# A hybrid mLSTM and attention layer: other queues and another order for its first loads

## The chip, the cores and the metric

The kernel runs on one core of one Trainium2 chip. The metric is the device time of an execution in microseconds; three executions of the kernel before took 302.65, 302.69 and 302.83 us, median 302.69. The core has five engines with instruction streams of their own: TensorE (PE in the profile; its weight loads are shown apart as PEld), VectorE (DVE), ScalarE (ACT), GpSimd (POOL) and SyncE (SP). Transfers are issued by SP, by POOL or by ACT and carried out by 16 DMA engines.

## The reference

One layer of a decoder with 512 tokens and a model width of 1024, all in float32:

```
h    = RMSNorm(x) * norm_w
proj = h @ w_in                       # 1024 -> 4616 columns, ten parts
mlstm: causal conv + SiLU on q and k, chunked matrix memory with gates, per-head norm, SiLU gate z (4 heads x 128)
moba:  QK-norm, ALiBi, block-sparse causal attention, SiLU gate z (8 heads x 64)
out  = x + concat(mlstm, moba) @ w_out
```

What the change touches lies at the very start: the first columns of `proj`, for which `x` (transposed) and the first weights have to be in on-chip memory.

## The kernel before

**Products in three parts.** Every float32 matrix is split into a high part (cast to the fp32r type, `whi` or `xh`) and the rest (`wlo` or `xl`). A product is three products on PE: high with high, `wlo` with `xh`, `whi` with `xl`. For the first weights, ACT makes `xh` as a copy scaled by `norm_w` (a column of the tile `sm`), DVE makes `xl` from the same raw tile, the same column and `xh`, and DVE makes both `whi` and `wlo` (later weights get `whi` from ACT). This is `split_x` and `g_split` with the loop over `kk` in lines 675 to 684; `kk = 0` is done in two halves, k = 0 and k = 1.

**The first stage.** The chunk called z (520 columns) is computed for all 512 tokens. Its order (line 1138) runs over k, 128 rows of the contraction each; for each k over the three part products; for each of these over four token tiles, two products each, one of 264 columns and one of 256. So a group is eight products on PE, and three groups make a k: (`whi`, `xh`), (`wlo`, `xh`), (`whi`, `xl`). Behind this stage follow the q and k projections by a scheme with seven block products instead of eight (m1 to m7), then the other projections mixed with the mLSTM and the attention work, then the output projection.

**The first loads.** `xraw` holds the transposed x in four tiles of two halves; `load_x(kk, u)` (line 642) loads half u of tile kk, 256 KB, and `load_w` (line 502) loads one piece of weights, with `between` as two halves of 260 KB with something else issued between them. All go through SP. The raw x tiles lie in `tq` and `tk`, which are used for something else later. `smalls` (31 KB: `norm_w`, convolution weights, gate biases and the like) goes into the tile `sm`.

**Warm-up and constants.** Ahead of all that, DVE clears a small matrix `zero` and a column `warm`, ACT runs one SiLU on `warm` (which brings a table load), and PE multiplies `zero` with itself ten times (lines 448 to 452). POOL scales one column of `sm` (line 594), then makes the identity `ident`, distances and other constants; DVE makes `sel`, four selection matrices of 36 x 128, from `ident` (lines 625 to 628).

**What sets the order.** Instructions given before `nc.on = True` (line 647) are issued in the order of the code, each on its engine. After that line the class `Schedule` collects every instruction with its engine, an estimated cost (`cost`, line 220) and its predecessors (by overlapping regions), and `issue` (line 348) places them by list scheduling: `place` gives each engine, when it is free, the most urgent instruction that is ready; urgencies come from a pass backwards through the graph; of the program order and twelve such rounds the order with the smallest planned span is taken. In this reckoning a transfer is an issue on SP (100 ns in `cost`), then a task on one resource `dma` at 1480 ns per 512 KB with a reserve factor of 1.5, then 3500 ns of latency; DVE and ACT costs have a factor of 1.06, a result passes to another engine in 400 ns, and on the same engine in 110 ns. What was issued before `nc.on` is not part of the graph and counts as there from the start.

Of the kernel before, what the change touches and what calls it, by code (L numbers as in the profile page):

```python
# [12 lines left out]
F32R = mybir.dt.float32r  # L13
AF = mybir.ActivationFunctionType
ALU = mybir.AluOpType
AX = mybir.AxisListType

P = 128
D = 1024
S = 512  # L20
NT = S // P
KT = D // P
MLH = 4
# [4 lines left out]
C_NW, C_CW, C_CB, C_MN, C_QW, C_KW, C_GB = 0, 8, 40, 48, 52, 53, 54  # L28
# [103 lines left out]
class Stage:  # L132
# [6 lines left out]
    def add(self, eng, cost, fn, after=(), at=0.0, lat=220.0, then=0.0):  # L139

        t = {"eng": eng, "cost": cost, "fn": fn, "after": [a for a in after if a], "at": at, "lat": lat,
             "then": then, "n": len(self.tasks)}
        self.tasks.append(t)
        return t
# [45 lines left out]
class Schedule:  # L190
# [29 lines left out]
    def cost(self, eng, name, out, ins, args, kw):  # L220
        n = 1
        for d in (args[1] if name == "tensor_reduce" else out).shape[1:]:
            n *= d
        if name.startswith("dma"):
            return 1000.0 if eng == "gpsimd" else 100.0
        if eng == "tensor":
            if name == "transpose":
                return 109.0
            n = 1
            for d in kw["rhs"].shape[1:]:  # L230
                n *= d
            if kw["rhs"].dtype == F32R:

                return (max(0.452 * n, 60.0) + 2.0) * (0.5 if kw["rhs"].shape[0] == 64 else 1.0)
            return max(n, 64) * 4 * (0.43 if out.shape[0] == P else 0.21)
        if eng == "scalar":
            c = 180.0 + 0.85 * n
            if name == "activation":
                c += 95.0 * sum(isinstance(kw.get(k), bass.AP) for k in ("scale", "bias"))
            return c + (190.0 if "accum_out" in kw else 0.0)  # L240
        if eng == "gpsimd":
            return 330.0 + 190.0 * n if kw.get("op") == ALU.pow else 500.0 + 1.05 * n
        if name == "tensor_tensor_scan":
            return 1210.0
        if name == "tensor_copy" and not any(r[0].startswith("bank") for r in ins):
            return 160.0 + 0.52 * n
        c = 155.0 + 1.04 * n
        if name == "scalar_tensor_tensor" and len(ins) > 2:
            c += 100.0
        return c + (83.0 if "accum_out" in kw else 0.0)  # L250
# [137 lines left out]
def hybrid_layer(ctx: ExitStack, tc: tile.TileContext, xT, x, w_in, w_out, smalls, out):  # L388
    nc = Schedule(tc.nc)
# [10 lines left out]
    def sb(name, shape, dtype=F32):  # L400
        return const.tile(shape, dtype, name=name)
# [35 lines left out]
        return tinies[:, ntiny[0] - n:ntiny[0]]  # L437

    sm = sb("sm", [P, NSMALL])
    nc.sync.dma_start(sm, smalls)  # L440


    rstdb = sb("rstdb", [P, S])
# [1 line left out]
    zero = rstdb[:, 0:256].bitcast(mybir.dt.bfloat16)  # L445
    warm = sb("warm", [P, 1])
    nc.vector.memset(warm, 0.0)
    nc.scalar.activation(warm, warm, AF.Silu)
    wb = banks.get()
    for _ in range(10):  # L450
        nc.tensor.matmul(wb, lhsT=zero[:, 0:P], rhs=zero, start=True, stop=True)
    banks.put(0.0, wb)

# [2 lines left out]
    for name, cols in _chunks():  # L456
        n = len(cols)
# [31 lines left out]
    def raw_room():  # L489
        turn["raw"] += 1  # L490
        return rawroom[(turn["raw"] - 1) % 3]
# [4 lines left out]
    def in_src(name, kk, n=512):  # L496
        return bass.AP(tensor=w_in.tensor, offset=w_in.offset + offs_w[name, kk], ap=[[2 * n, P], [1, 2 * n]])

    def pair(t, n):
        return t[:, :2 * n].rearrange("p (k n) -> p k n", k=2)  # L500

    def load_w(dst=None, between=None):
        if not lseq or (dst is None and nout[0] >= 3):
            return
        i = lseq.pop(0)
        name, kk, n = pieces[i][:3]
        if dst is None:
            nout[0] += 1
            dst = raw_room()
        src = in_src(name, kk, n)  # L510
        if between:
            nc.sync.dma_start(dst[:, :n], src[:, :n])
            between()
            nc.sync.dma_start(dst[:, n:2 * n], src[:, n:])
        else:
            nc.sync.dma_start(dst[:, :2 * n], src)
        raws[i] = (dst, pair(dst, n))
# [73 lines left out]
        plan.until(lambda: (name, kk) in W)  # L591
        return W[name, kk]

    nc.gpsimd.tensor_scalar(sm[64:128, C_QW:C_QW + 1], sm[64:128, C_QW:C_QW + 1], 2.0, 0.0, op0=ALU.mult, op1=ALU.add)


    ident = sb("ident", [P, P])
    make_identity(tc.nc, ident)
# [9 lines left out]


    sz = sb("sz", [P, NT, 512])  # L610
    tq = sb("tq", [P, NT, 512])
    tk = sb("tk", [P, NT, 512])
    vbuf = sb("vbuf", [P, NT * MLH * 129])
    tv = vbuf[:, :NT * 512].rearrange("p (t n) -> p t n", t=NT)
    mv = vbuf.rearrange("p (t h e) -> p t h e", t=NT, h=MLH)
# [6 lines left out]
    emcol = sb("emcol", [P, NT, 4])  # L622
    mrow2 = sb("mrow2", [36, S], F32R)
    nc.gpsimd.memset(mrow2.bitcast(F32), 0.0)
    sel = sb("sel", [36, MLH, P], F32R)
    for h in range(MLH):
        nc.vector.tensor_tensor(sel[:, h], ident[0:36, h:h + 1].to_broadcast([36, P]),
                                ident[0:36, 32 + h:33 + h].to_broadcast([36, P]), op=ALU.add)
    xpt = sb("xp", [P, 2, S + 4])
    nc.gpsimd.memset(xpt[:, :, 0:3], 0.0)  # L630
    xps = Bufs(plan, [xpt[:, i] for i in range(2)])
# [2 lines left out]
        return cv[c // 2][:, c % 2] if c < 4 else tq[:, c - 4]  # L634


    flat = lambda ap: ap.rearrange("p a n -> p (a n)")
    xraw = [flat(tq)[:, 0:1024], flat(tq)[:, 1024:2048], flat(tk)[:, 0:1024], flat(tk)[:, 1024:2048]]
    xtok = [vbuf[:, 1024 * (t % 2):1024 * (t % 2) + 1024] for t in range(NT)]
    zb = [b5.get() for _ in range(4)]  # L640

    def load_x(kk, u):
        nc.sync.dma_start(xraw[kk][:, u * 512:(u + 1) * 512],
                          bass.AP(tensor=xT.tensor, offset=xT.offset + kk * P * 1024 + u * 512,
                                  ap=[[1024, P], [1, 512]]))

    nc.on = True
    load_x(0, 0)
    load_w(zb[0], lambda: load_x(0, 1))
    for kk in range(1, 4):  # L650
        load_w(zb[kk])
        for u in range(2):
# [22 lines left out]
    for kk in range(4):  # L675
# [6 lines left out]
        for _ in split:  # L682
            pass
        nsplit[0] += 1
    xtmp = [t[:, 0:1024] for t in zb]
    plan.now = act.clock = dve.clock = 5500.0


# [429 lines left out]
    def pe_task(cost, fn, after=()):  # L1118
        nonlocal pe_last
        pe_last = st.add("PE", cost, fn, [pe_last, *after], lat=0.0)  # L1120
        return pe_last
# [100 lines left out]
    for m in PAIR:  # L1222
        for j in range(8):
            a, k = (j // 4, j % 4) if m in ("m6", "m7", "m4") else (j % 2, j // 2)
# [181 lines left out]
    for r in range(2):  # L1406
        for c in range(2):
            t = b5.get()
# [81 lines left out]
    for n, name in enumerate(NAMES):  # L1490
        if name not in SUMS:
            continue
        tag, other, op = SUMS[name]
# [136 lines left out]
```

## Time and profile before

| | us |
|---|---|
| profiled execution, whole | 302.68 |
| its span, first to last instruction | 301.0 |
| median of three runs | 302.69 |
| PE busy | 296.0 (98% of the span) |
| DVE busy | 214.9 (71%) |
| ACT busy | 169.6 (56%) |
| POOL busy | 67.1 (22%) |
| share of PE in the chain that ended last | 97% |

How to read it: busy time counts the execution of instructions, not waits and not the issue of transfers. The span begins with the first recorded instruction, so 1.68 us of the execution lie outside it. Matmuls are pipelined and their ends are modelled, so the start of a matmul or of a weight load is a safer number than its end. The chain is followed back from the last instruction to whatever released each step.

### The profile page before, as it was taken

The page shows a single profiled execution, that of the slowest core. Times are in us where ns is not written, and L with a number is a line of the kernel's source. Part 1 is how long each engine was busy: PE and PEld are TensorE (multiplying, and loading weights), DVE is VectorE, ACT ScalarE, POOL GpSimd, SP SyncE. Part 2 cuts the span into 40 slices and gives each one's busy share as a digit, 9 for nine tenths or more (in the row PEclk, how much of TensorE's full clock was granted, in tenths as well). Part 3 has the DMA queues.
Part 4 walks back from the last instruction along what each step waited for, and adds up shares of the span by engine and source line. Part 5 has one row for each costly group of instructions (what it writes and reads, how often), then busy time and mean ns, then how long its engine had stood idle before and what let it go on. Part 6 is the DMA issues. An engine that isn't in the chain of part 4 may idle for free.

```text
span 301.0 us, 4348 instructions
## 1 busy us (share of the span) xinstructions
PE 296.0 (98%) x1566; PEld 234.9 (78%) x1566; DVE 214.9 (71%) x457; ACT 169.6 (56%) x309; POOL 67.1 (22%) x90
## 2 busy tenths in 40 slices
PE   8999999999999999999999999999999999999995
PEld 3999888888887667767776668888889988888884
DVE  4886996789697675986686784372046767899992
ACT  3685749875537854364554599377032525779500
POOL 4000202149900344002561031000101037121200
PEclk9999999999999999999999999999999999999998
DMA  7994785643134200240001601465518399964434
GB/s 203 396 415 186 191 237 148 121 138 114 58 111 140 71 2 0 70 142 1 1 3 70 209 2 70 70 207 154 131 42 212 102 286 255 247 112 74 71 127 153
DMA packets 13381, 40.19 MB, mean 134 GB/s; under 512 B 1584, under 2 KB 1840, under 8 KB 13360
## 3 DMA queue, kind: packets, MB, share of 16 engines
q1 hardware_dynamic: 10640, 32.05, 30.6%
q0 software_dynamic: 2720, 7.87, 15.3%
q8 instruction: 12, 0.20, 0.3%
q14 instruction: 9, 0.07, 0.1%
HBM read 37.81 MB, written 2.10 MB: 133 GB/s over the span
## 4 chain that ended last, share of the span: by engine, by line
PE 97%; DMA 1%; DVE 0%; SPq 0%; issue 0%
PE bank L258 97%; DMA b<-in_w_in_dram 1%; DVE whi L258 0%; DVE b L258 0%; SPq L258 0%; SPq L381 0%
## 5 line engine op out<-in xcount | busy, mean ns | idle before, releaser
L258 PE MATMUL bank<-wlo,xh 128*128 128x512 f32 (+2 forms) x220 | 71.3, 358 | 0.0
L258 PE MATMUL bank<-whi,xl 128*128 128x512 f32 (+2 forms) x220 | 71.1, 359 | 0.0
L258 PE MATMUL bank<-whi,xh 128*128 128x512 f32 (+2 forms) x220 | 70.9, 362 | 0.1
L258 DVE TENSOR_TENSOR wlo<-raw,whi 128x1024 fp32r<-128x1024 f32 x35 | 42.5, 1218 | 22.3 <-ACT whi L258 22.2
L258 PEld LDWEIGHTS bank<-whi,xh 128*128 128x128 f32 x220 | 38.1, 188 | 8.1 <-ACT xh L258 1.0
L258 PEld LDWEIGHTS bank<-wlo,xh 128*128 128x128 f32 x220 | 38.3, 188 | 6.6 <-issue 0.2
L258 PEld LDWEIGHTS bank<-whi,xl 128*128 128x128 f32 x220 | 38.3, 188 | 6.4
L258 ACT CAST whi<-raw 128x1024 fp32r<-128x1024 f32 x35 | 36.5, 1049 | 11.6 <-PE bank L258 11.5
L258 PE MATMUL bank<-xh,whi 128*128 128x512 f32 x96 | 40.8, 425 | 0.0
L258 PE MATMUL bank<-xl,whi 128*128 128x512 f32 x96 | 39.4, 410 | 0.0
L258 PE MATMUL bank<-xh,wlo 128*128 128x512 f32 x96 | 38.7, 403 | 0.0
L258 PE MATMUL bank<-whi,br 128*128 128x512 f32 x112 | 35.9, 397 | 0.0
L258 POOL TENSOR_SCALAR b<-b,tinies 128x128 f32<-128x128 f32 (+3 forms) x32 | 20.0, 632 | 35.1 <-DVE tinies L258 32.5
L258 PEld LDWEIGHTS bank<-whi,br 128*128 128x128 f32 x112 | 21.0, 188 | 5.0
L258 ACT ACTIVATE b<-b,tinies 128x128 f32<-128x128 f32 (+3 forms) x32 | 17.8, 556 | 11.3 <-DVE tinies L258 11.0
L258 DVE CUSTOM_DVE_ANT_0 b<-bank,b 128x128 f32<-128x128 f32 (+3 forms) x32 | 14.8, 483 | 10.7 <-PE bank L258 10.7
L258 PEld LDWEIGHTS bank<-xh,whi 128*128 128x128 f32 x96 | 18.1, 188 | 5.5 <-issue 1.4
L258 PE MATMUL bank<-wlo,br 128*128 128x512 f32 x56 | 22.2, 400 | 0.0
L258 PEld LDWEIGHTS bank<-xh,wlo 128*128 128x128 f32 x96 | 18.1, 188 | 3.8 <-issue 0.2
L258 PEld LDWEIGHTS bank<-xl,whi 128*128 128x128 f32 x96 | 18.1, 189 | 3.6 <-issue 0.7
L258 POOL TENSOR_TENSOR tinies<-tinies,mhalf 128x8 f32<-128x8 f32 (+1 forms) x12 | 18.9, 1589 | 6.3 <-DVE tinies L258 6.2
L258 PE MATMUL bank<-ident,b 128*128 128x128 f32 (+1 forms) x104 | 19.0, 267 | 0.0
(170 smaller groups left out, 457.2 us busy)
## 6 DMA issues: line engine op xcount, KB each, us to landing
raw<-in_w_in_dram SPq DMA_DIRECT2D x28, 512.0 KB, 3.4
raw<-in_w_out_dram SPq DMA_DIRECT2D x5, 512.0 KB, 4.4
vbuf<-in_x_dram SPq DMA_DIRECT2D x4, 512.0 KB, 7.8
out_dram<-b SPq DMA_DIRECT2D x7, 256.0 KB, 2.1
b<-in_w_in_dram SPq DMA_DIRECT2D x3, 520.0 KB, 7.1
raw<-in_w_out_dram POOLq DMA_DIRECT2D x3, 512.0 KB, 6.3
b<-in_x_dram POOLq DMA_DIRECT2D x6, 256.0 KB, 4.4
tq<-in_xT_dram SPq DMA_DIRECT2D x4, 256.0 KB, 4.9
```

Source lines behind the costliest of these rows:

```text
L258: call = lambda: fn(*args, **kw)
```

## The change

Five edits, all in the first loads. The first x tile half is issued from ScalarE before the SiLU, ahead of the planner's part. On SP the first half of the first weights comes first in the code, then `smalls`, the second x half and the second half of the weights; all other loads follow as before. The POOL instruction on `sm` and the building of `sel` move behind `nc.on = True`, so that the planner places them. Eight warm-up products are issued instead of ten. And the planner's cost of issuing a DMA on an engine other than GpSimd is 450 ns instead of 100, for the whole kernel. `tq`, `tk`, `flat` and `xp` are only declared at another place, and an unused name goes.

```diff
-            return 1000.0 if eng == "gpsimd" else 100.0
+            return 1000.0 if eng == "gpsimd" else 450.0
...
     sm = sb("sm", [P, NSMALL])
-    nc.sync.dma_start(sm, smalls)
...
     nc.vector.memset(warm, 0.0)
+    tq, tk = sb("tq", [P, NT, 512]), sb("tk", [P, NT, 512])
+    flat = lambda ap: ap.rearrange("p a n -> p (a n)")
+    nc.scalar.dma_start(flat(tq)[:, 0:512], bass.AP(tensor=xT.tensor, offset=xT.offset, ap=[[1024, P], [1, 512]]))
     nc.scalar.activation(warm, warm, AF.Silu)
     wb = banks.get()
-    for _ in range(10):
+    for _ in range(8):
         nc.tensor.matmul(wb, lhsT=zero[:, 0:P], rhs=zero, start=True, stop=True)
...
-    nc.gpsimd.tensor_scalar(sm[64:128, C_QW:C_QW + 1], sm[64:128, C_QW:C_QW + 1], 2.0, 0.0, op0=ALU.mult, op1=ALU.add)
-
     ident = sb("ident", [P, P])
...
+    nc.on = True
+    load_w(zb[0], lambda: (nc.sync.dma_start(sm, smalls), load_x(0, 1)))
     sel = sb("sel", [36, MLH, P], F32R)
     for h in range(MLH):
         nc.vector.tensor_tensor(sel[:, h], ident[0:36, h:h + 1].to_broadcast([36, P]),
                                 ident[0:36, 32 + h:33 + h].to_broadcast([36, P]), op=ALU.add)
...
-    nc.on = True
-    load_x(0, 0)
-    load_w(zb[0], lambda: load_x(0, 1))
     for kk in range(1, 4):
         load_w(zb[kk])
         for u in range(2):
...
+    nc.gpsimd.tensor_scalar(sm[64:128, C_QW:C_QW + 1], sm[64:128, C_QW:C_QW + 1], 2.0, 0.0, op0=ALU.mult, op1=ALU.add)
     plan.now = act.clock = dve.clock = 5500.0
```

## Rows read from the trace of the kernel before

**Rows 1.** Chain that ended last, in order of time: start us, us, what

```profile
1.70 3.43 DMA b<-in_w_in_dram
...
5.16 0.54 DVE whi L258
...
5.83 291.52 PE bank L258 x1556
```

**Rows 2.** Waits of PE's weight loads, whole span: us in total, times, longest us

```profile
PEld bank L258 <- issue: 12.0, 42, 0.8
PEld bank L258 <- DVE tinies L258: 1.8, 5, 0.4
...
PEld bank L258 <- ACT b L258: 1.4, 4, 0.4
```

**Rows 3.** SP from 0 to 18 us: start, us, instruction, count, idle before and releaser

```profile
0.79 0.39 SPq L381 DMA_DIRECT2D sm<-in_smalls_dram  x1
1.24 0.42 SPq L258 DMA_DIRECT2D tq<-in_xT_dram  x1
1.70 0.42 SPq L258 DMA_DIRECT2D b<-in_w_in_dram  x1
```

**Rows 4.** ACT from 0 to 18 us

```profile
0.79 1.28 ACT L381 ACT_TABLE_LOAD   x1 [0.79 <-PEq L1618]
...
4.55 0.72 ACT L258 ACTIVATE xh<-tq,sm 128x512 fp32r<-128x512 f32 x1 [2.27 <-DMA tq<-in_xT_dram]
5.84 0.72 ACT L258 ACTIVATE xh<-tq,sm 128x512 fp32r<-128x512 f32 x1 [0.57 <-DMA tq<-in_xT_dram]
9.69 1.43 ACT L258 ACTIVATE xh<-tq,sm 128x512 fp32r<-128x512 f32 x2 [3.12 <-DMA tq<-in_xT_dram]
```

**Rows 5.** DVE from 0 to 18 us

```profile
3.52 0.89 DVE L381 TENSOR_TENSOR sel<-ident 36x128 fp32r<-36x128 f32 x4 [2.33 <-POOL ident masks.py:199]
5.16 0.53 DVE L258 CAST whi<-b 128x520 fp32r<-128x520 f32 x1 [0.74 <-DMA b<-in_w_in_dram]
5.61 0.73 DVE L258 SCALAR_TENSOR_TENSOR xl<-tq,sm,xh 128x512 fp32r<-128x512 f32 x1
6.26 0.69 DVE L258 TENSOR_TENSOR wlo<-b,whi 128x520 fp32r<-128x520 f32 x1
...
9.05 0.70 DVE L258 CAST whi<-b 128x1040 fp32r<-128x1040 f32 x1 [0.48 <-DMA b<-in_w_in_dram]
```

**Rows 6.** PE from 0 to 18 us: products, merged by group

```profile
1.24 4.45 PE L381 MATMUL bank<-rstdb 128*128 128x512 bf16 x10 [1.24 <-DVE warm L381]
5.83 1.24 PE L258 MATMUL bank<-whi,xh 128*128 128x264 f32 x8
7.01 1.22 PE L258 MATMUL bank<-wlo,xh 128*128 128x264 f32 x8
8.07 1.12 PE L258 MATMUL bank<-whi,xl 128*128 128x264 f32 x8
...
11.91 1.12 PE L258 MATMUL bank<-whi,xh 128*128 128x264 f32 x8
```

**Rows 7.** DMA issues by line: count, size of one, median us from issue to landing

```profile
sm<-in_smalls_dram SPq DMA_DIRECT2D x1, 31.0 KB, 1.8
```

**Rows 8.** PE's weight loads from 0 to 18 us, the third and the tenth

```profile
1.65 0.15 PEld L381 LDWEIGHTS <-rstdb 128*128 128x128 bf16 x1 [0.28 <-issue]
...
4.63 0.15 PEld L381 LDWEIGHTS <-rstdb 128*128 128x128 bf16 x1 [0.28 <-issue]
```

**Rows 9.** Windows: us, busy (count) of PE, PEld, DVE, ACT, POOL, PEclk, DMA share, GB/s

```profile
0.00:5.83 5.83, 4.45 (x10) 1.37 (x11) 1.84 (x8) 2.21 (x3) 3.04 (x14) 1.00 0.61 179
...
20.00:25.00 5.00, 5.00 (x43) 5.00 (x43) 2.76 (x7) 1.47 (x3) 0.00 (x0) 1.00 1.03 418
```

**Rows 10.** POOL from 0 to 18 us

```profile
2.68 0.18 POOL L381 TENSOR_SCALAR sm<-sm 64x1 f32<-64x1 f32 x1 [2.18 <-DMA sm<-in_smalls_dram]
```

**Rows 11.** The tile sel: its readers, ns min/median/max, first to last start us

```profile
L258 PEld LDWEIGHTS bank<-mrow,sel x4: 182/183/186, 170.7 to 172.7; 36*128 36x128 f32 x4
```

More of the change, by code (lines that the diff above doesn't have):

```diff
@@ L610, in hybrid_layer @@
     sz = sb("sz", [P, NT, 512])
-    tq = sb("tq", [P, NT, 512])
-    tk = sb("tk", [P, NT, 512])
     vbuf = sb("vbuf", [P, NT * MLH * 129])
@@ L624, in hybrid_layer @@
     nc.gpsimd.memset(mrow2.bitcast(F32), 0.0)
[L625 to L628, printed above, removed]
     xpt = sb("xp", [P, 2, S + 4])
@@ L634, in cvt @@
         return cv[c // 2][:, c % 2] if c < 4 else tq[:, c - 4]
-    flat = lambda ap: ap.rearrange("p a n -> p (a n)")
     xraw = [flat(tq)[:, 0:1024], flat(tq)[:, 1024:2048], flat(tk)[:, 0:1024], flat(tk)[:, 1024:2048]]
@@ L647, in hybrid_layer @@
     nc.on = True
-    load_x(0, 0)
-    load_w(zb[0], lambda: load_x(0, 1))
+    load_w(zb[0], lambda: (nc.sync.dma_start(sm, smalls), load_x(0, 1)))
+    sel = sb("sel", [36, MLH, P], F32R)
+    for h in range(MLH):
+        nc.vector.tensor_tensor(sel[:, h], ident[0:36, h:h + 1].to_broadcast([36, P]),
+                                ident[0:36, 32 + h:33 + h].to_broadcast([36, P]), op=ALU.add)
     for kk in range(1, 4):
@@ L684, in hybrid_layer @@
         nsplit[0] += 1
-    xtmp = [t[:, 0:1024] for t in zb]
+    nc.gpsimd.tensor_scalar(sm[64:128, C_QW:C_QW + 1], sm[64:128, C_QW:C_QW + 1], 2.0, 0.0, op0=ALU.mult, op1=ALU.add)
     plan.now = act.clock = dve.clock = 5500.0
```

## The prediction

> **What bounds the kernel now.** I read the chain of waits in order of time first. One unbroken PE piece runs from 5.83 us for 291.52 us of the 301.0, and what stands ahead of it is a DMA issue, 3.43 us of a transfer and one DVE cast [rows 1]. Then I looked for waits inside the piece: the table of what PE's weight loads waited for has no transfer in it, only small items, 3.2 us in 9 pieces for DVE and ACT results beside 12.0 us for which no engine is named [rows 2]. So PE's stream of products is a block of fixed length behind a start-up, and any change to the start-up is worth what it moves the block.
>
> Next I read the start-up engine by engine. SP issues one DMA every 0.46 us: `sm` at 0.79, the first x tile at 1.24, the first half of the first weights at 1.70, and the second x tile in the slot after [rows 3]. The x tile has landed when ACT begins its cast `xh`, at 4.55, the second when the next begins, at 5.84 [rows 4]. The weights land at 5.13 (1.70 + 3.43), DVE casts `whi` from 5.16 to 5.69 [rows 1, 5], and the first product stands at 5.83, 0.14 us later [rows 6]. `xh` was done at 5.27, so the weights decided. The first group of eight products (`whi`, `xh`) is followed at 7.01 by the second (`wlo`, `xh`), and the groups then settle at one every 0.96 us (four of them from 8.07 to 11.91, [rows 6]). The second group came later than 5.83 + 0.96 = 6.79, because DVE finished `wlo` at 6.95: it had put `xl` (5.61 to 6.34) ahead of it [rows 5]. The real anchor of the block is thus 7.01.
>
> **The change part by part.** The time of the profiled execution is 302.68 us, 1.68 more than its span, and the median of the runs is 302.69, so I sum against 302.68.
>
> *Weights first on SP.* Issue goes from 1.70 to 0.79, 0.91 us earlier. If the transfer takes its 3.43 us again, it lands at 4.22. But x tile and weights now start at the same moment, and before they needed 3.89 us together (1.24 to 5.13): at worst 0.79 + 3.89 = 4.68. Both ends come from [rows 1, 3]; I take the middle, 4.45.
>
> *The x tile from ScalarE's queue.* ACT's first instruction, a table load, starts at 0.79 [rows 4]; the DMA issue goes ahead of it and costs ACT some 0.42 us (SP's row for one DMA, [rows 3]). The table load then ends near 2.5 instead of 2.07, a small activation behind it; ACT idles until 4.55 today, so that is hidden, and would cost only if the data came before that. The tile lands between 4.10 (0.45 earlier) and 4.68.
>
> *`sm` behind the weights.* This is the edit with a price. `xh` and `xl` are scaled by columns of `sm`, which today lies ready at 2.59 (0.79 + 1.8, [rows 7]), and which is now issued at about 1.25, behind 260 KB of weights. Alone it would be there at 3.05; treated like the second x tile, which landed 0.71 after the weights ahead of it (5.84 less 5.13), at 5.16. By size (31 of 256 KB of that 0.71, hence 0.09) I take 4.45 + 0.09 = 4.54, nearest to that row scaled. The Trainium skill's page "DMA: Bandwidth & Descriptors", section "Queues, rings and completion order", says that each DMA engine works off one queue's descriptors in ring order and alternates between the queues that have work. No row here shows two hardware queues at once; by it `sm` waits for all the weights ahead of it while the x tile shares with them, which would put all three at about 4.68 to 4.77 and the gain 0.2 us below mine.
>
> *First product.* ACT casts `xh` from 4.54 to 5.26 (0.72, [rows 4]); `whi` is ready at 4.48 + 0.53 = 5.01, so ACT, not DVE, is late now. With the same 0.14 us to PE: 5.40, or 0.43 earlier.
>
> *The second group.* The planner that orders the instructions puts `xl` ahead of `wlo` today because in its own reckoning the x tile is there 1.1 us before the weights and `wlo` must wait 110 ns behind `whi`, while `xl` is ready. With the x tile out of the plan and `sm` behind the weights it reckons `whi` done at 5.53, `wlo` ready at 5.64, `xl` at 6.36, so `wlo` goes first. Then `wlo` is done at 5.01 + 0.69 = 5.70, before it is wanted at 5.40 + 0.96 = 6.36. The gain there is 7.01 - 6.36 = 0.65. Should `xl` stay first: 5.26 + 0.73 + 0.69 = 6.68, plus the 0.06 to PE, 6.74: 0.27.
>
> *Eight warm-up products.* Ten run from 1.24 to 5.69 [rows 6], 0.426 apart (seven steps of their weight loads from 1.65 to 4.63, [rows 8]); eight end 0.85 earlier, at 4.84. With ten, PE could not have begun at 5.40, so this edit makes the gain possible. What it risks is the clock. The granted clock reads 1.00 in the start-up too [rows 9], but 512 columns in 0.426 us are 1.2 GHz, and products of 264 columns in 0.12 us (0.96 for eight) are 2.4 GHz. The tenth warm-up product still started at the slow level (near 5.07) and the real ones at 5.83 were fast: the rise lay between. Where it lies late in that stretch, my first products run slow until then: at most 0.43 us at half speed, 0.2; I charge 0.05.
>
> *`sel` later, and the POOL scaling of `sm`.* Four DVE instructions (0.89 us) at 3.52 wait for `ident`, which POOL makes only after waiting until 2.68 for `sm` [rows 5, 10]. Without that wait `ident` is there some 1.9 us earlier and `sel` ends well before 4.4. Its first reader is at 170.7 [rows 11]. Cost nothing; if it landed behind `whi` it would cost 0.89 of DVE in the only stretch where DVE is close. The moved POOL instruction takes 0.18 us [rows 10], and POOL then has nothing in the window from 20 to 25 us [rows 9], so it hides.
>
> *What is late next.* Every later load keeps its place in SP's order and is issued one slot (0.46) earlier. The seventh group (k = 2) starts at 11.91 and had `whi` at 9.75, both kept waiting by transfers, `xh` at 10.41 [rows 4 to 6]: 1.5 us of slack, more than any gain here, and its transfers move too. The stream keeps the DMA engines full to 25 us [rows 9], so it shifts as a whole.
>
> *The planner's 450 instead of 100 ns per SP DMA* can reorder instructions in the whole kernel. Its bounds are the waits of PE that exist, 3.2 us in 9 pieces of up to 0.4 [rows 2]: one more or one less, +-0.4.
>
> Sum: -0.65 + 0.05 = -0.60, so 302.68 - 0.60 = 302.08. Bounds from the parts: weights and `sm` at 4.22 and 4.31 give 5.17, 6.13 and a gain of 0.88; `sm` at 5.16 gives 6.02, 6.98 and a gain of 0.03, below nothing with the clock's 0.2.
>
> **The rivals.**
> 1. *The clock rises late.* The warm-up stops at 4.84, before the rise of today (after 5.07), and PE then idles until 5.40, where the gap was 0.14. If the chip wants its activity anew, the products run at 1.2 GHz from 5.40 for as long as the rise took from 1.24, 3.83 to 4.59 us. A group takes 8 x 264/1.2 = 1.76 instead of 0.96, so 46% of that is lost: 1.75 to 2.1. Time: 302.08 + 1.75 to 2.1, about 304.0, slower. It decides from where the rise needs the last two products. For it: ten products were still slow. Against: PE is busy from 1.24 to 4.84 and again from 5.40. The Trainium skill's page "TensorE: Matmul & The Clock Gate", section "What's actually happening", states that "the default state is throttled, and activity releases the throttle"; the trace agrees (slow at 1.24, fast at 5.83), and whether eight products are activity enough no row here shows.
> 2. *`sm` takes the place of the wait removed*, or `xl` stays ahead of `wlo`: gain 0 to 0.3, 302.4 to 302.7. For it: `sm` is 31 KB over 128 partitions, so many small packets, and no row shows such a tile behind a full queue. Against: it is an eighth of an x tile.
> 3. *The change doesn't do what it says*: ACT's table load (1.28) stays ahead of its DMA. Issue at 2.1, tile at 5.4, `xh` at 6.1, second group at 7.2: +0.2, 302.9. Against: the load belongs to the activation behind it.
> 4. *Another order later in the kernel* gives or takes a wait or two: 301.6 or 302.8.
>
> **How the numbers follow.** Forecast 0.60, with its own range 301.7 to 302.5; rival 1 0.18; rival 2 0.13; rival 3 0.03; rival 4 0.06. About 0.2% (0.6 us, so 302.09 and 303.29) is what a measurement of this kernel can tell from no change, and the forecast sits at that edge: a little over half of it counts as faster (0.35), since its bounds leave about as much on either side; rival 4's better half and the luckier part of rival 2's uncertain price make it 0.40. Slower is rival 1 and a little of 4: 0.20. Same takes 0.40. The range reaches from 301.6 to 303.9, into rival 1, leaving out its dearer part.
>
> **What would show it.** Right: an ACT DMA at 0.79 and SP's weights at 0.79; `xh` beginning near 4.5 and just behind the landing of `sm`; `wlo` ahead of `xl` on DVE; first product near 5.4, second group near 6.36, groups 0.96 apart at once; and the PE block as long as before (291.5). Wrong: products of 264 columns 0.22 apart behind 5.4 (rival 1); `xh` at 5 or later with ACT waiting for `sm` (rival 2); the ACT DMA behind 2 us (rival 3); a PE block of another length (rival 4).

## The result, and the profile after

The changed kernel takes 305.15 us (median of eight executions), the kernel before 302.74 beside it: ratio 1.006, interval 1.0031 to 1.0089. It is slower, where 302.08 was forecast. The eight executions fall into two groups with nothing between them: three at 303.12 to 303.21 and five at 305.13 to 305.49. The profiled execution took 305.49, 2.81 more than that of before, with a span of 303.8.

The start of the new order came as planned. SP and ACT from 0 to 9 us (start, us, instruction, idle before and releaser), to be held against [rows 3, 4]:

```profile
0.79 0.39 SPq L258 DMA_DIRECT2D b<-in_w_in_dram  x1
1.23 0.42 SPq L258 DMA_DIRECT2D sm<-in_smalls_dram  x1
```

```profile
0.79 0.41 ACTq L381 DMA_DIRECT2D tq<-in_xT_dram  x1
1.22 1.28 ACT L381 ACT_TABLE_LOAD   x1 [1.22 <-PEq L1614]
...
4.70 1.50 ACT L258 ACTIVATE xh<-tq,sm 128x512 fp32r<-128x512 f32 x2 [1.98 <-DMA sm<-in_smalls_dram]
```

The x tile's DMA stands ahead of the table load, `xh` now waits for `sm`, and on DVE `wlo` stands ahead of `xl`, against [rows 5]:

```profile
4.23 0.43 DVE L258 CAST whi<-b 128x520 fp32r<-128x520 f32 x1 [1.95 <-DMA b<-in_w_in_dram]
4.70 0.73 DVE L258 TENSOR_TENSOR wlo<-b,whi 128x520 fp32r<-128x520 f32 x1
5.45 0.75 DVE L258 SCALAR_TENSOR_TENSOR xl<-tq,sm,xh 128x512 fp32r<-128x512 f32 x1
```

The products are another matter. PE from 0 to 18 us, merged by group, against [rows 6]:

```profile
1.24 3.60 PE L381 MATMUL bank<-rstdb 128*128 128x512 bf16 x8 [1.24 <-DVE warm L381]
5.47 2.10 PE L258 MATMUL bank<-whi,xh 128*128 128x264 f32 x8 [0.63 <-DVE wlo L258]
7.37 1.94 PE L258 MATMUL bank<-wlo,xh 128*128 128x264 f32 x8
9.10 1.80 PE L258 MATMUL bank<-whi,xl 128*128 128x264 f32 x8
10.74 1.14 PE L258 MATMUL bank<-whi,xh 128*128 128x264 f32 x8
...
16.51 1.11 PE L258 MATMUL bank<-whi,xh 128*128 128x264 f32 x8
```

The first product is at 5.47, 0.36 earlier than before (its releaser is given as `wlo`, done at 5.43; what it needs is `xh`, done at 5.42). But the first three groups start 1.90, 1.73 and 1.64 us apart and only the later ones 0.96. The window table, its columns as in [rows 9], has for the slow stretch:

```profile
5.47:10.70 5.23, 5.23 (x24) 5.23 (x25) 5.01 (x8) 2.39 (x4) 0.01 (x1) 1.00 1.00 367
```

24 products in 5.23 us are 0.218 each; 264 or 256 columns in 0.218 us are 1.2 GHz. The column of the granted clock (the last but two) reads 1.00 all the same. It did so in the slow start-up of before, too [rows 9]; the level there has to be read from the pace of the products. The tenth group starts at 16.51, and at 14.79 in the trace of before: 1.72 us later.

The rest is lost far from the edit. The chain that ended last, which before held one unbroken PE piece [rows 1]:

```profile
0.79 3.42 DMA b<-in_w_in_dram
...
5.47 261.84 PE bank L258 x1409
...
267.81 0.90 issue
268.71 1.05 ACT whi L258
...
271.57 1.08 DVE wlo L258
...
275.74 2.29 DVE wlo L258 x2
...
278.07 22.09 PE bank L258 x106
```

PE's block ends at 300.16 instead of 297.35, so 2.81 later in all: 1.72 by the tenth group and 1.09 behind it, of which 0.90 is one wait of PE for `wlo`:

```profile
278.07 0.51 PE L258 MATMUL bank<-wlo,xh 128*128 128x512 f32 x1 [0.90 <-DVE wlo L258]
```

ACT in that stretch, first before, then after:

```profile
262.72 0.63 ACT L258 ACTIVATE cv<-cv 128x512 f32<-128x512 f32 x1
...
265.10 0.60 ACT L258 ACTIVATE b<-bank 128x512 f32<-128x512 f32 x1 [1.46 <-PE bank L258]
...
267.41 1.06 ACT L258 CAST whi<-raw 128x1024 fp32r<-128x1024 f32 x1
...
270.70 1.05 ACT L258 CAST whi<-vbuf 128x1024 fp32r<-128x1024 f32 x1
```

```profile
265.90 0.60 ACT L258 ACTIVATE b<-bank 128x512 f32<-128x512 f32 x1 [2.99 <-PE bank L258]
266.39 0.62 ACT L258 ACTIVATE cv<-cv 128x512 f32<-128x512 f32 x1
...
268.71 1.05 ACT L258 CAST whi<-vbuf 128x1024 fp32r<-128x1024 f32 x1 [0.90 <-issue]
...
270.50 1.04 ACT L258 CAST whi<-raw 128x1024 fp32r<-128x1024 f32 x1
```

Two pairs have changed places. `whi<-vbuf` now stands ahead of `whi<-raw` and waits 0.90 us (the profile names nothing that releases it), and `b<-bank` ahead of `cv<-cv`, waiting 2.99 us for PE. ACT works its instructions off in their order, so what stands behind a waiting one waits too: `whi<-raw` comes at 270.50 instead of 267.41, 3.1 us later, of which 1.7 is the shift of the start.

Theory from this: two losses, independent of each other. A: PE stands still for 0.63 us behind the shorter warm-up, in some executions the clock then stays at 1.2 GHz until some 10.7 us, and that costs 2.2 us (305.38 against 303.20, the medians of the two groups). B: the planner's 450 ns changed the order on ACT some 260 us later, and that costs 1.09 (the expectations below reckon with 1.05). Rivals: the slow stretch comes from the new queues (ACT's transfer, `sm`) and not from PE's pause; the late wait comes from the earlier start or from DVE's own order.

### The profile page after: what moved, and what is told of

It is laid out like the page before. It is cut to its first block, busy times and chain, and to the rows that moved or that the text cites. A ratio compares the mean times of both kernels' runs of the same rounds, so it can differ in the third digit from the quotient of the medians.

```text
span 303.8 us, 4340 instructions
## 1 busy us (share of the span) xinstructions
PE 297.4 (98%) x1564; PEld 236.3 (78%) x1564; DVE 215.6 (71%) x457; ACT 169.0 (56%) x309; POOL 70.2 (23%) x90
## 4 chain that ended last, share of the span: by engine, by line
PE 93%; DVE 3%; DMA 1%; ACT 1%; issue 0%
PE bank L258 93%; DVE wlo L258 1%; DMA b<-in_w_in_dram 1%; ACT whi L258 1%; DVE raw L258 0%; DVE xl L258 0%; DVE b L258 0%; ACT xh L258 0%; ACT b L258 0%; DVE whi L258 0%; ACT br L258 0%
## 5 line engine op out<-in xcount | busy, mean ns | idle before, releaser
L258 PE MATMUL bank<-whi,xh 128*128 128x512 f32 (+2 forms) x220 | 71.9, 368 | 0.6 <-DVE wlo L258 0.6
L258 PE MATMUL bank<-whi,xl 128*128 128x512 f32 (+2 forms) x220 | 71.9, 364 | 0.0
L258 PEld LDWEIGHTS bank<-whi,xh 128*128 128x128 f32 x220 | 38.9, 193 | 8.4 <-ACT xh L258 1.5
L258 PEld LDWEIGHTS bank<-wlo,xh 128*128 128x128 f32 x220 | 39.0, 193 | 7.5 <-DVE wlo L258 1.3
L258 POOL TENSOR_SCALAR b<-b,tinies 128x128 f32<-128x128 f32 (+3 forms) x32 | 21.7, 684 | 35.6 <-DVE tinies L258 32.5
L258 POOL TENSOR_TENSOR tinies<-tinies,mhalf 128x8 f32<-128x8 f32 (+1 forms) x12 | 19.9, 1677 | 6.2 <-DVE tinies L258 6.0
```

Of the source, the lines that this page charges most:

```text
L258: call = lambda: fn(*args, **kw)
```

## The experiments

**Ten warm-ups in the changed kernel**, then eight in the kernel before.

```diff
-    for _ in range(8):
+    for _ in range(10):
```

> The changed kernel with ten warm-up products instead of eight; nothing else differs. Theory A (the clock): with eight products TensorE idles from 4.84 to 5.47 us and its clock then rises near 10.6 in some executions; with ten it rises before the first real product in all of them. Expected: products of 264 columns 0.12 us apart from the first, no execution near 305.3, all within 0.3 us; the start gains little, since ten products end at 5.69 (second group near 6.8, 0.2 earlier than 7.01), and the stall near 277 us stays: 302.74 - 0.2 + 1.05 = 303.6. Rival B (the moved loads are what costs, not the warm-up): slow products behind 5.4 and two kinds of executions as in the changed kernel, median 305.2.

303.55 us (nine executions, 303.23 to 303.82), ratio 1.0023 (1.0014 to 1.0033): one group, none at 305. The late wait was still there (ACT's 0.90 at 265.83). Loss A goes with the warm-up, loss B doesn't.

```diff
-    for _ in range(10):
+    for _ in range(8):
```

> The kernel before with eight warm-up products; nothing else differs. Theory A (the clock): warm-up ends at 4.84, the first real product stands at 5.83, a gap of 1.0 us, longer than in the changed kernel, so the low clock is met at least as often: executions of two kinds, near 302.7 and near 304.7 (1.7 to 2.2 more), the profile at one of them. Rival B (warm-up count does nothing): 302.74, all within 0.3 us.

302.74 us, ratio 1.0014 (0.9999 to 1.0029): eight of twelve at 302.60 to 302.88, four at 304.02 to 304.63. The old queues with the short warm-up have the two groups as well, so the new transfers aren't needed for A.

**The planner's cost alone**, undone in the changed kernel, then done in the kernel before.

```diff
-            return 1000.0 if eng == "gpsimd" else 450.0
+            return 1000.0 if eng == "gpsimd" else 100.0
```

> The changed kernel with the planner's 100 ns per DMA of SP instead of 450; nothing else differs. Theory C (the 450 reorders the output projection and makes the stall near 277 us): the stall of 0.90 us before a wlo,xh product is gone, and the two kinds of executions lie 1.05 lower than the changed kernel's, near 302.1 and 304.3. Rival D (the stall comes from the moved instructions, which the planner sees in another place): stall stays, 303.2 and 305.3.

303.03 us, ratio 1.0032 (1.0013 to 1.0051): seven at 302.88 to 303.04, five at 304.81 to 305.25. The two groups are there, 0.9 and 0.6 above what I expected. The wait at 278 had gone, but a new one had come. ACT and PE of this kernel:

```profile
48.01 0.62 ACT L258 CAST br<-b 128x512 fp32r<-128x512 f32 x1 [0.96 <-PE bank L258]
48.54 1.99 ACT L258 CAST whi<-b 128x1024 fp32r<-128x1024 f32 x2
```

```profile
49.63 1.19 PE L258 MATMUL bank<-whi,br 128*128 128x512 f32 x4 [0.50 <-ACT whi L258]
```

`br<-b` waits 0.96 us for PE ahead of `whi<-b`, and PE waits 0.50 us for the latter; in the trace of before `whi<-b` went first:

```profile
47.55 1.05 ACT L258 CAST whi<-b 128x1024 fp32r<-128x1024 f32 x1
48.62 0.62 ACT L258 CAST br<-b 128x512 fp32r<-128x512 f32 x1
```

The old number doesn't bring the old order back, since the graph is another (`sm`, `sel` and the scaling of `sm` are in it, the first x tile isn't). What was wrong in my expectation is that 450 alone makes the bad order; another new plan did, too. From the tenth group on this kernel lost 0.81 us against before; 0.50 of it is this wait, where the rest lies I didn't look for.

```diff
-            return 1000.0 if eng == "gpsimd" else 100.0
+            return 1000.0 if eng == "gpsimd" else 450.0
```

> The kernel before with the planner's 450 ns per DMA of SP; nothing else differs. Theory C (450 makes the late stall): a PE wait near 277 us and 302.74 + 1.05 = 303.8, all executions within 0.3 us, first products fast. Rival D: no such wait, 302.7.

303.89 us (303.80 to 304.00), ratio 1.0037 (1.0024 to 1.005). With the old start untouched, the same 0.90 on ACT (266.13) and the same late wait came. The whole is 1.08 us. In its profiled execution PE's block ends 1.13 later than before: 0.95 of it came behind the tenth group, which is loss B by itself, and 0.18 ahead of it, where the first weights took 3.73 us to land, against 3.43 before. Nothing in the edit touches that transfer.

**The pause filled.** Five products of 128 columns behind the eight: at the slow level a quarter of 0.426 us each, 0.53 together, so that they end by 4.84 + 0.53 = 5.37 and delay no product.

```diff
         nc.tensor.matmul(wb, lhsT=zero[:, 0:P], rhs=zero, start=True, stop=True)
+    for _ in range(5):
+        nc.tensor.matmul(wb[:, 0:P], lhsT=zero[:, 0:P], rhs=zero[:, 0:P], start=True, stop=True)
```

> The changed kernel with its eight warm-up products followed by five narrow ones (128 columns instead of 512), so that TensorE works on to about 5.2 to 5.4 us where it idled from 4.84 to 5.47; nothing else differs. Theory A (the idle gap ahead of the first real products is what leaves the clock low): no execution near 305.3, all near the faster kind of the changed kernel, 303.1 to 303.3, with the stall near 277 us still in. Rival E (the number or the columns of the warm-up products count, not the gap: 8 x 512 + 5 x 128 is less than 10 x 512): two kinds of executions remain, 303.2 and 305.3, the slow kind perhaps rarer.

303.36 us (twelve executions, 303.18 to 303.96), ratio 1.002 (1.0009 to 1.0031). One group. PE of its profiled execution:

```profile
1.24 3.86 PE L381 MATMUL bank<-rstdb 128*128 128x512 bf16 x13 [1.24 <-DVE warm L381]
5.48 1.22 PE L258 MATMUL bank<-whi,xh 128*128 128x264 f32 x8 [0.38 <-ACT xh L258]
6.54 1.12 PE L258 MATMUL bank<-wlo,xh 128*128 128x264 f32 x8
```

First product as in the changed kernel, 0.96 us per group from the second on. Theory A holds: with work in the pause there is no slow stretch of 5 us. What is left, 303.36, is loss B with the start's gain off it.

**The order of before kept, with the new start.** The planner reckons as before and the plan is the old one; only what is issued differs: x tile from ACT, weights then `sm` on SP, `wlo` ahead of the first `xl`, eight and five warm-ups.

```diff
+    nc.scalar.dma_start(flat(tq)[:, 0:512], bass.AP(tensor=xT.tensor, offset=xT.offset, ap=[[1024, P], [1, 512]]))
...
+    nc.sync.dma_start(zb[0][:, :520], in_src("z", 0, 520)[:, :520])
+    nc.sync.dma_start(sm, smalls)
...
+            nc.ops[n]["fn"] += late["fn"]
+            late["fn"] = []
```

> The order of before kept for everything behind the first loads (the planner sees what it saw before, 100 ns, sel and the x tile included), and by hand: the first x tile from ScalarE's queue, the first weights and then sm from SyncE's, wlo ahead of the first xl on VectorE, eight warm-up products and five narrow ones. Theory (start gains 0.5, the planner's new order loses 1.05): second group near 6.45 as in the changed kernel's plan, no wait behind it, 302.8 - 0.5 = 302.3 in all executions. Rival F (the start's gain is given back later whatever the order): 302.8.

302.30 us, ratio 0.9982 (0.9971 to 0.9994), PE's block unbroken for 291.70 us from 5.52. The new start is worth something once neither loss is bought with it.

The same without the five narrow products:

```diff
-    for _ in range(5):
-        nc.tensor.matmul(wb[:, 0:P], lhsT=zero[:, 0:P], rhs=zero[:, 0:P], start=True, stop=True)
```

> The kernel that keeps the order of before, with the eight warm-up products of the change and none of the narrow ones, so that TensorE stands still for about 0.6 us ahead of the first product. Theory (the pause decides the clock): two kinds of executions, about 302.3 and about 304.3 us, the second in a third to two thirds of them. Rival (the slow kind comes from the change's other order of instructions): one kind at 302.3.

302.18 us, ratio 1.0003 (0.9986 to 1.0021): eight of twelve at 302.06 to 302.21, four at 303.67 to 304.25. The two groups follow the pause in a fourth kernel. And the lower group is what I had forecast for the start: PE of its profiled execution (302.09 us):

```profile
1.24 3.59 PE L381 MATMUL bank<-rstdb 128*128 128x512 bf16 x8 [1.24 <-DVE warm L381]
5.45 1.24 PE L258 MATMUL bank<-whi,xh 128*128 128x264 f32 x8 [0.62 <-DVE wlo L258]
6.53 1.12 PE L258 MATMUL bank<-wlo,xh 128*128 128x264 f32 x8
```

The same eight warm-ups in the same 3.6 us and the same pause as in the profile of the changed kernel, and here the products are fast at once. So the pause makes the slow stretch possible, and something that varies between executions decides.

**`sm` from GpSimd's queue**, with 8 and 4 warm-ups, to take it out from behind the weights; then with `xl` ahead of `wlo`.

```diff
-    nc.sync.dma_start(sm, smalls)
+    nc.gpsimd.dma_start(sm, smalls)
```

> As the kernel with the order of before kept, but sm is issued from GpSimd's queue at the very start and not behind the weights, and four narrow warm-up products instead of five. Theory (sm behind the weights cost 0.3 of the start): xh begins when the x tile lands, near 4.4 instead of 4.70; first product near 5.2, second group near 6.2, 302.8 - 0.75 = 302.05. Rival G (sm on a third queue still lands with the weights, since all share the DMA engines): xh at 4.7 and 302.3.

304.23 us, ratio 1.0034 (1.0018 to 1.0051), three of twelve at 302.59 to 302.77 and nine at 304.09 to 304.58. A miss by 2.2 us. Its DMA issues (count, size, median us from issue to landing) and PE:

```profile
sm<-in_smalls_dram POOLq DMA_DIRECT2D x1, 31.0 KB, 4.4
```

```profile
1.24 4.02 PE L381 MATMUL bank<-rstdb 128*128 128x512 bf16 x12 [1.24 <-DVE warm L381]
6.49 2.10 PE L258 MATMUL bank<-whi,xh 128*128 128x264 f32 x8 [1.23 <-ACT xh L258]
8.39 1.77 PE L258 MATMUL bank<-wlo,xh 128*128 128x264 f32 x8
```

Issued at 1.33, `sm` landed at 5.7: later than behind the weights on SP. The warm-up ran to 5.26, longer than in the filled kernel (to 5.10) and one narrow product shorter than in the old plan's (to 5.37), but a pause of 1.23 us followed, and nine of twelve were of the upper group: more than with eight products. So it isn't the amount of warm-up that decides (rival E); more of it doesn't help if the pause stays.

> As the kernel with sm from GpSimd's queue, but with the first xl ahead of wlo on VectorE, as the kernel before has it. Theory (the order of these two sets the second group): first product near 5.2 again, second group at 5.13 + 0.73 + 0.69 + 0.06 = 6.6, 0.4 later than with wlo first: 302.4. Rival (the order makes no difference): 302.05.

304.23 us, ratio 1.0036 (1.002 to 1.0052), a miss for the same reason: first product at 6.71, eight of twelve at 303.93 or more. Its profiled execution (304.90) shows loss A in another form. PE by groups, and one line of the window table:

```profile
6.71 1.24 PE L258 MATMUL bank<-whi,xh 128*128 128x264 f32 x8 [1.45 <-ACT xh L258]
8.11 1.69 PE L258 MATMUL bank<-wlo,xh 128*128 128x264 f32 x8 [0.16 <-DVE wlo L258]
9.59 1.94 PE L258 MATMUL bank<-whi,xl 128*128 128x264 f32 x8
```

```profile
9.59:11.33 1.74, 1.74 (x10) 1.74 (x10) 1.71 (x3) 1.07 (x2) 0.00 (x0) 0.50 1.02 394
```

After a pause of 1.45 us the first group ran at 2.4 GHz, and then the clock fell: the granted clock reads 0.50 here, and the eight products from 9.59 to 11.33 are 0.218 us apart, the pace of 1.2 GHz. Of the order of `xl` and `wlo` the run tells nothing. Hence the next two, on the kernel that keeps the order of before.

```diff
     load_w(zb[0], second_x)
...
-            late = nc.ops[-1]
-            n = len(nc.ops)
...
-            nc.ops[n]["fn"] += late["fn"]
-            late["fn"] = []
```

> The kernel that keeps the order of before, with xl ahead of wlo on DVE, as the kernel before has them. The prediction gave the new order 0.4 us of the second group's start. If so, the second group starts at about 7.1 to 7.4 us instead of 6.97 and the time is 302.5 to 302.7. Rival: the second group is bound by the pace of the first, then 302.3 as without the swap.

302.61 us, ratio 0.9996 (0.9987 to 1.0004); second group at 7.12. It has the expected time, 0.31 more than with `wlo` first. In its profiled execution PE didn't wait for `wlo` (done at 6.81), since the first group was still slow; in an execution with the fast level at 5.47 it would have had to, for some 0.3 us (5.47 + 1.07 = 6.54). That is argued, no trace shows it; the spread fits: 302.51 to 302.79 here, 302.08 to 302.94 with `wlo` first.

```diff
-    nc.sync.dma_start(zb[0][:, :520], in_src("z", 0, 520)[:, :520])
     nc.sync.dma_start(sm, smalls)
+    nc.sync.dma_start(zb[0][:, :520], in_src("z", 0, 520)[:, :520])
```

> The kernel that keeps the order of before, with the small tensors issued ahead of the first weights on SP instead of behind them (0.79 and about 1.24 us). If the wait for the small tensors is what the order on SP costs, xh is written at about 4.4 us, the first product is at about 5.3, the second group at about 6.3 to 6.8, and the time is 302.1 us. Rival: the weights land later by what the small tensors land earlier, and the time stays at 302.3. It tells the prediction's step 'the small tensors land at 4.54 behind the weights' from a queue without order.

302.46 us, ratio 0.9992 (0.9983 to 1.0): no gain, as the rival had it. ACT's `xh` begins at 4.18, with the x tile, but now DVE is late:

```profile
4.83 0.43 DVE L258 CAST whi<-b 128x520 fp32r<-128x520 f32 x1 [2.55 <-DMA b<-in_w_in_dram]
```

The weights lose the slot that `sm` takes, 0.44 us, and land 0.60 later (4.81). Its first product was still at 5.41 and the second group at 6.44, up to 0.1 earlier than with the weights first. That was lost again at the fifth group, which waited for the `wlo` made from the second half of the weights (cast at 6.64 in the kernel with eight warm-ups):

```profile
7.84 0.43 DVE L258 CAST whi<-b 128x520 fp32r<-128x520 f32 x1 [1.18 <-DMA b<-in_w_in_dram]
```

Its tenth group started at 14.51, in the kernel with the old plan and eight warm-ups at 14.18. `sm`, though first on SP, took 3.1 us to land, against 1.8 before [rows 7], when ACT issued no transfer.

**Loss B instruction by instruction**, on the filled kernel. First the cast `whi<-vbuf` alone (`v` in the code; the lines that find it are left out), then the activation `cv<-cv` as well (`c`, put ahead of the eviction `b<-bank`, `b`); all else stands as the planner put it.

```diff
+        to = whi[whi.index(v) + 2]
+        order.remove(v)
+        order.insert(order.index(to) + 1, v)
```

> The changed kernel with the narrow extra warm-up products, and one ACT instruction moved: the cast of the cross product's input (whi<-vbuf) is issued two casts of that engine later, everything else in its place. If that one cast, which waits 0.9 us for TensorE at 267.8 us at the head of ACT's in-order queue, is the whole of the late loss, the pause of TensorE near 277 us goes and the time falls from 303.4 to about 302.4 us. Rival: the other instructions that the longer planning moved cause it too; then a pause of 0.5 to 0.9 us stays there and the time is 303.1 to 303.4.

303.00 us, ratio 1.001 (1.0002 to 1.0019): between the two expectations. PE's late pause fell from 0.90 to 0.50. PE, ACT and DVE:

```profile
275.56 0.50 PE L258 MATMUL bank<-wlo,xh 128*128 128x512 f32 x1 [0.50 <-DVE wlo L258]
```


```profile
263.97 0.60 ACT L258 ACTIVATE b<-bank 128x512 f32<-128x512 f32 x1 [2.98 <-PE bank L258]
264.46 0.62 ACT L258 ACTIVATE cv<-cv 128x512 f32<-128x512 f32 x1
```

```profile
265.12 0.69 DVE L258 TENSOR_TENSOR cv<-cv,ot 128x512 f32<-128x512 f32 x1 [1.24 <-ACT cv L258]
```

DVE stands idle 1.24 us for `cv`, behind ACT's wait for PE, and has no gap of more than 0.1 from there to the `wlo` that PE waits for.

```diff
+        order.remove(c)
+        order.insert(max([order.index(b)] + [order.index(j) + 1 for j in self.ops[c]["pre"] if j in order]), c)
```

> As the run with the moved cast, and one more ACT instruction moved, by one place: the in-place activation cv<-cv now stands ahead of the eviction b<-bank that waits 2.98 us for TensorE, instead of behind it; all else is as it was. Theory: the half of the late loss that the moved cast left (a pause of 0.50 us at 275.56) comes from that wait in ACT's in-order queue, through DVE's idle 1.24 us ahead of cv<-cv,ot; then the pause goes and the time is 302.4 to 302.5 us. Rival: it comes from the order on DVE itself (raw<-raw,vbuf ahead of wlo); then the pause stays and the time is 303.0.

302.26 us, ratio 0.9979 (0.997 to 0.9988), faster than both kernels. The chain has one PE piece again, and on ACT `cv<-cv` stands ahead of the waiting `b<-bank`:

```profile
5.49 291.42 PE bank L258 x1556
```

```profile
261.76 0.63 ACT L258 ACTIVATE cv<-cv 128x512 f32<-128x512 f32 x1 [0.78 <-DVE cv L258]
263.95 0.60 ACT L258 ACTIVATE b<-bank 128x512 f32<-128x512 f32 x1 [1.56 <-PE bank L258]
```

Two ACT instructions were loss B: 303.36 to 303.00 to 302.26, 1.10 us together. The traces say it without the spread of the start. From the start of the tenth group to the end of PE's block it is 282.56 us in the kernel before and 282.56 or 282.57 in all seven others with the old plan; 283.65 to 283.67 in the changed kernel, filled and with ten warm-ups too; 283.08 with the first instruction moved and 282.34 with both. DVE's order, which the planner had changed too and which stayed changed, costs nothing; what is left of the new plan is even 0.22 shorter than the old.

## Why the prediction was wrong

**Weights, x tile and `sm`: right.** Weights landed at 4.21 (forecast 4.45, bounds 4.22 to 4.68): 3.42 us, as long as before, when the x tile went ahead of them on the same queue. The x tile, issued by ACT, landed at about 4.4. `sm` landed at about 4.65 (forecast 4.54), and ACT, free since 2.72, began `xh` at 4.70, some 0.3 later than the x tile would have allowed. Giving `sm` the place ahead of the weights won nothing (302.46 against 302.30). The Trainium skill's page "DMA: Bandwidth & Descriptors", section "Queues, rings and completion order", by whose ring order and alternation the prediction estimated 4.68 to 4.77 for all three, comes near the trace for `sm` (4.65) and not for the weights (4.21) or the x tile (4.4).

**First and second group: right where the clock is up, the size in part by luck.** First product 5.40 forecast, 5.47 measured (5.41 to 5.52 in the filled kernels and those with the old plan and `sm` on SP). Second group 6.36 forecast, 6.53 and 6.54 measured where the products were fast from the start: the first group took 1.06 to 1.08 us there, not the 0.96 that I reckoned, so the second gained 0.48 and not 0.65. But a group behind a wait took 1.06 in the kernel before as well (7.01 to 8.07 [rows 6]), which I had also counted as 0.96, so the third group gained 0.58. PE's block ended at 296.74 in the kernel with the old plan and eight warm-ups, 297.35 before: the gain was 0.61, forecast 0.60. The two slips cancelled for the most part, and the 0.05 for the clock did the rest. `wlo` went ahead of `xl` as reckoned; with `xl` first 0.31 of it is lost.

**`sel` and POOL's scaling: right.** `sel` ran at 1.39, 2.1 us earlier than before, and no product waits for it.

**"I charge 0.05" for the clock: wrong, the larger failure.** The term was 2.2 us in five of eight executions (305.38 against 303.20). Rival 1 had the mechanism, the place and nearly the price (1.75 to 2.1), and 0.18 of the chance. The failing step was to take the rise at the instant that it had in the one trace of before, between 5.07 and 5.83, for all executions and also for a PE that stands still there; so the dearest case was 0.43 us at half speed, where the runs showed three groups at 1.2 GHz. The instant varies: the same 13 warm-up products took 4.13 us in the profile of the kernel with the old plan, where the first group was still slow (5.52 to 6.97), 3.86 in the filled kernel and 3.50 in the one with `sm` first, where the rise came inside the warm-up. The page "TensorE: Matmul & The Clock Gate" of the Trainium skill, section "What's actually happening", says that activity releases the throttle; the runs agree: with PE at work right up to the first real product, the second group was fast in every profile here. Where PE stood still between 4.84 and 5.47, the profiled execution of the changed kernel had the fast pace only from some 10.6 us on.

That the median lies as high as 305.15 is a matter of the draw: five of eight. With the four of twelve of the kernel with the old plan it would have been about 303.2, and the median would have shown loss B alone.

| kernel | warm-ups | they took, us | pause ahead of the first product, us | of the upper group |
|---|---|---|---|---|
| before | 10 | 4.45 | 0.14 | 1 of 120 |
| before, planner's cost 450 | 10 | 3.79 | 1.00 | 0 of 5 |
| changed, ten warm-ups | 10 | 4.45 | none | 0 of 9 |
| changed, filled | 8 + 5 | 3.86 | 0.38 | 0 of 12 |
| the same, one and two instructions moved | 8 + 5 | 4.13 | 0.04 and 0.12 | 0 of 22 |
| old plan, new start | 8 + 5 | 4.13 | 0.15 | 0 of 12 |
| the same, `xl` first | 8 + 5 | 4.13 | 0.10 | 0 of 11 |
| the same, `sm` first on SP | 8 + 5 | 3.50 | 0.67 | 0 of 11 |
| changed | 8 | 3.60 | 0.63 | 5 of 8 |
| changed, planner's cost 100 | 8 | 3.26 | 0.96 | 5 of 12 |
| old plan, new start | 8 | 3.59 | 0.62 | 4 of 12 |
| before, eight warm-ups | 8 | 3.33 | 1.22 | 4 of 12 |
| `sm` from GpSimd | 8 + 4 | 4.02 | 1.23 | 9 of 12 |
| the same, `xl` first | 8 + 4 | 4.02 | 1.45 | 8 of 12 |

Warm-up and pause are those of the profiled execution alone. Where the rise came inside the warm-up, the products ended sooner and the pause is longer; in five such profiles (3.26 to 3.86 us, pauses of 0.38 to 1.22) the products behind it were fast at once. That a pause behind the rise does no harm isn't shown by that: with `sm` from GpSimd and `xl` first the clock was up behind the pause and then fell.

Filling the pause has a small price, as far as the profiles show. With 13 products the first group was still slow for a part in four of six profiles (1.38 to 1.65 us instead of 1.06), and the filled kernels spread over 0.3 to 0.9 us, where the lower group with eight products spreads over 0.1 to 0.3.

**"The planner's 450: +-0.4": mis-sized, with the wrong bound.** I bounded it by the waits that PE has in the trace before [rows 2]. A new order isn't bound by those: it makes new ones. It measured +1.08 alone in the kernel before (0.95 of it behind the tenth group) and 1.09 in the changed one. Rival 4 was this, with 0.06 of the chance and 302.8 where 303.2 came.

**The sum, corrected:** 302.68 - 0.61 + 1.09 = 303.16, the lower group (303.12 to 303.21); with the slow stretch, the tenth group 1.72 later instead of 0.61 earlier, 305.49, the profiled execution.

Left open: what sets the instant of the rise in an execution, why the clock fell behind a fast group in one of them, and why `sm` takes 4.4 us from GpSimd's queue.

## What to carry to other kernels

Keep TensorE at work right up to the first real product, with narrow products that are over by then even at 1.2 GHz: a pause of 0.6 us and more there cost 1.3 to 2.2 us in a third to three quarters of the executions of six kernels, and one profile doesn't show how often. When a list scheduler's cost changes, or what it has in its graph, compare each engine's order with the old one over the whole kernel and look for instructions that wait and so hold back what stands behind them on their engine; two of them cost more here than the edit gained. Edits that come together are worth timing apart: here the new start alone gained 0.5 us, and two parts that looked like trimmings took back 1.1 and, in five of eight executions, another 2.2.

## What the runs showed of the hardware

- The level of TensorE's clock in the first microseconds varies between executions of one kernel. The granted clock read 1.00 in stretches ahead of the first rise where the products' pace was 1.2 GHz, and 0.50 where the clock fell after it.
- Behind a pause of 1.45 us TensorE ran one group fast and then fell to 1.2 GHz, while it was at work.
- The first group of eight products behind a wait took 1.03 to 1.08 us at 2.4 GHz, the later ones 0.96.
- The same 31 KB, issued first on SP, took 1.8 us to land when no other engine issued a transfer [rows 7] and 3.1 beside 256 KB issued by ACT; 3.4 behind 260 KB on SP; and 4.4 from GpSimd's queue beside two other queues, whose issue also took 0.74 us of GpSimd against 0.42 on SP.
- 260 KB issued by SP, beside 256 KB issued by ACT at the same moment, landed in 3.42 us; third on SP, behind 31 and 256 KB, they took 3.43, and 3.73 in the profile of a kernel with the same first loads. What they take alone no run shows.
